# Four sums of weight blocks per seven-product pair: from VectorE subtractions to adding DMAs out of DRAM

## The chip, the core and the metric

The kernel runs on one core of one Trainium2 chip. The metric is the device time of one execution in microseconds (us). The engines named below are TensorE (PE; its weight loads PEld), VectorE (DVE), ScalarE (ACT), GpSimd (POOL) and SyncE (SP). SP only issues loads; POOL issues a few DMAs and does small masks. All arithmetic data is f32; matmul operands are f32 numbers that were rounded to the matmul's own format (`fp32r`).

## What is computed

A two-layer decoder trunk on 256 positions (two tiles of 128) with model width 2048. Layer 0 is a gMLP mixer, layer 1 a stick-breaking attention, each with a norm ahead, a residual add behind and a gate from the same input projection. Nearly all the work is in four products of the 256 x k activations with large weight matrices:

```python
proj = xn @ w_in                       # layer 0: 2048 -> 3*4096  (u | v | gate)
uv = jax.nn.gelu(proj[..., :2 * GMLP_WIDTH]); zg = proj[..., 2 * GMLP_WIDTH:]
...                                    # v: norm, causal mixing over positions
y = u * mixed * jax.nn.silu(zg)
h = h + y @ w_out                      # layer 0: 4096 -> 2048
proj = rms_norm(h) @ w_in              # layer 1: 2048 -> 4*2048  (q | k | v | gate)
...                                    # stick-breaking attention, 16 heads of 128
h = h + (o * jax.nn.silu(zg)) @ w_out  # layer 1: 2048 -> 2048
```

## The kernel before, in words

**Cutting.** Every weight tile comes from DRAM as f32 and is cut into two fp32r tiles: ACT copies it to `hi` (line 106), DVE subtracts `raw - hi` into `lo` (line 108). A product is then three matmuls, hi*hi, hi*lo and lo*hi (lines 112 to 114). There are five buffers of `hi` and five of `lo`, so the cutting can run at most five tiles ahead of PE.

**Pairs.** The two input projections run in pairs of column blocks of 512 (`Pair`). Of a pair's 16 k-tiles of 128 rows, 2*ks (ks is 4, in the gate/u stage 3) are taken by a Strassen-Winograd scheme: the 2x2 blocks left (2 row tiles by 2 k-groups) times right (2 k-groups by 2 column blocks) need seven block products, p1 to p7, in place of eight. The right-hand blocks b11, b12, b22, b21 are `ks` tiles of 128 x 512 each; they lie in SBUF in groups of two tiles (a group is 128 x 1024, with ks = 3 the second one is 128 x 512). The scheme needs four sums of right-hand blocks. `minus` (line 213) makes each on DVE, in place, one instruction a group. The left-hand sums s1 to s4 are made once a layer (`sums`). The other k-tiles of the pair are done plainly in `column(0)` and `column(1)`: one tile of 128 x 1024 is cut and used by twelve matmuls.

There are 19 pairs: v (3, layer 0, ks 4), gu (8, layer 0, ks 3), then in layer 1 qk (4), bv (2) and bg (2), with ks 4. The stages o (layer 0's output) and f (layer 1's) do plain products.

**Order.** `run` writes `head` (p1 and p5) in turn with the steps of the last pair's `column(1)`, then `body` (p6, p2, p7, p3, p4), then `column(0)`. A Tile scheduler with a timeline of its own sets the final order on each engine; each engine then takes its instructions strictly in that order. A load of a right-hand block into its buffer waits until the block's last reader in the pair before is done. The columns have three raw buffers (`wraw`). SP issues all these loads.

**Banks.** p1 goes to bank a, then b starts from a copy of a, p6 adds to b, c starts from a copy of b, and so on; an `es` tile on the side holds p5, which DVE adds to b and c (lines 243 and 250).

**Names in the rows.** `gu_b` is both a right-hand block (SBUF) and a bank (PSUM) of a gu pair; `gu_p_hi` and `gu_p_lo` are the cut of a block for one of the seven products; `gu_raw`, `gu_hi` and `gu_lo` belong to the columns; `vg` and `ws` are small tiles of layer 0's mixing, `gf` the last norm's gain. In the orders below the numbers stay on: `gu5_b00` is block b11 of pair gu5, `b01` is b12, `b11` is b22, `b10` is b21, and the last digit is the group.

Of the kernel before, what the change touches and what calls it, by code (L numbers as in the profile page):

```python
# [11 lines left out]
AF = mybir.ActivationFunctionType  # L12
ALU = mybir.AluOpType
# [11 lines left out]
def trunk_kernel(ctx: ExitStack, tc: tile.TileContext, x, xt, gcols, wst, a_w_in, a_v_norm_g,  # L25
# [11 lines left out]
    nc = tc.nc  # L37
# [45 lines left out]
    def f(ap):  # L83
        return ap.bitcast(F32)
# [31 lines left out]
    class Left:  # L116
# [10 lines left out]
        def sums(self, ks, out, name):  # L127

            full = []
            for i in range(2):  # L130
                sl = slice(i * ks, (i + 1) * ks)
                fl = sraw.tile([P, 4, S], F32, tag=f"b1{i + 1}_1", name=f"{name}_full{i}")
                nc.vector.tensor_add(fl[:, 0:ks], f(self.hi[:, sl, :]), f(self.lo[:, sl, :]))
                full.append(fl)
            a11, a12 = full[0][:, 0:ks, 0:P], full[1][:, 0:ks, 0:P]
            a21, a22 = full[0][:, 0:ks, P:S], full[1][:, 0:ks, P:S]
            sm = [sraw.tile([P, 2, 4, P], F32, tag=f"b2{i + 1}_1", name=f"{name}_sm{i}") for i in range(2)]
            s1, s2, s3, s4 = sm[0][:, 0, 0:ks], sm[0][:, 1, 0:ks], sm[1][:, 0, 0:ks], sm[1][:, 1, 0:ks]
            nc.vector.tensor_add(s1, a21, a22)
            nc.vector.tensor_sub(s3, a11, a21)  # L140
            nc.vector.tensor_sub(s2, s1, a11)
            nc.vector.tensor_sub(s4, a12, s2)
            for i, si in enumerate((s1, s2, s3, s4)):
                nc.scalar.copy(out[:, 0, i], si)
                nc.vector.tensor_sub(out[:, 1, i], si, f(out[:, 0, i]))
            self.s, self.ks = out, ks
# [32 lines left out]
    class Pair:  # L179
# [28 lines left out]
                tick(1)  # L208
                yield

        def minus(self, into, b0, b1):
            for g in range(len(self.groups)):
                nc.vector.tensor_sub(into[g], b0[g], b1[g])  # L213

        def head(self):
            left = self.left
            self.b11, self.b12 = self.load(0, 0), self.load(0, 1)
            self.a = self.bank("a")
            yield from self.block(self.b11, lambda k: left.part(k, 0), self.a, "p1", True)
            self.b22, self.b21 = self.load(1, 1), self.load(1, 0)  # L220
            self.minus(self.b11, self.b12, self.b11)
            self.e = self.bank("e")
            yield from self.block(self.b11, lambda k: left.sum_part(0, k), self.e, "p5", True)
            self.minus(self.b11, self.b22, self.b11)

        def body(self):
            left, off = self.left, self.left.ks
            b11, b12, b22, b21 = self.b11, self.b12, self.b22, self.b21
# [8 lines left out]
            nc.scalar.copy(es, e)  # L237
# [103 lines left out]
    left = Left(x_hi, x_lo)  # L341
# [87 lines left out]
    with ExitStack() as lg:  # L429
# [428 lines left out]
```

## Time and profile before

| | |
|---|---|
| median of 2 runs | 1185.88 us (1185.8 to 1185.95) |
| profiled execution | 1186.77 us, of which the profile's span is 1185.0 us |
| granted TensorE clock, mean | 0.995 |
| busy: PE, DVE, ACT, POOL | 1161.3, 945.3, 773.3, 40.6 us |
| DMA | 235.88 MB, mean 199 GB/s |
| subtractions of line 213 | 152 (v 24, gu 64, qk 32, bv 16, bg 16) |

The stages on the time axis: the first v products to about 60 us, the v pairs to about 160, gu pairs to about 510, stage o to about 720, the pairs of layer 1 to about 1080, stage f to the end. "DMA share" is the mean busy share of the core's 16 DMA engines. q1 is the queue that the loads go through, q0 the one of the DMAs that POOL issues.

### The profile page before, as it was taken

What the parts mean: (1) busy time and instruction counts of PE and PEld (TensorE: products, weight loads), DVE (VectorE), ACT (ScalarE), POOL (GpSimd) and SP (SyncE); (2) the same over time, 40 slices, a digit from 0 to 9 for tenths busy, and PEclk for the clock granted to TensorE, in tenths of its full rate; (3) what the DMA queues carried; (4) which work ended last, traced back from release to release, by engine and by line L of the source; (5) the groups of instructions that cost most, each with busy time, mean ns of one, the idle gap of its engine ahead of it and who ended that gap; (6) DMA issues with size and microseconds to landing.
All of it is one profiled execution on the core that took longest, in us unless ns stands there. A gap on an engine that the chain in (4) does not pass through costs nothing.

```text
span 1185.0 us, 14870 instructions
## 1 busy us (share of the span) xinstructions
PE 1161.3 (98%) x5393; PEld 961.3 (81%) x5393; DVE 945.3 (80%) x1050; ACT 773.3 (65%) x996; POOL 40.6 (3%) x55
## 2 busy tenths in 40 slices
PE   8799999999999999999999999999999999999997
PEld 6578888888888888888888887888888888878887
DVE  7599889989888887976556469899899989896564
ACT  6567668677676766766444456588679687885442
POOL 0200000110000000000000000001000000000000
PEclk9899999999999999999999999999999999999999
DMA  7975666675676566467555686475564564526662
GB/s 249 313 245 162 213 216 186 192 231 186 180 226 216 170 216 212 124 203 249 186 185 187 231 274 209 157 240 166 163 231 151 184 207 146 185 72 223 254 220 102
DMA packets 119609, 235.88 MB, mean 199 GB/s; under 512 B 7920, under 2 KB 12144, under 8 KB 119024
## 3 DMA queue, kind: packets, MB, share of 16 engines
q1 hardware_dynamic: 117648, 229.67, 59.5%
q0 software_dynamic: 1168, 4.20, 1.4%
q10 hardware_dynamic: 720, 1.07, 0.2%
q8 instruction: 42, 0.69, 0.2%
q14 instruction: 31, 0.25, 0.1%
HBM read 230.71 MB, written 4.19 MB: 198 GB/s over the span
## 4 chain that ended last, share of the span: by engine, by line
PE 78%; DVE 8%; ACT 6%; issue 4%; DMA 4%; SPq 0%; POOL 0%; POOLq 0%; DVEq 0%; ACTq 0%
PE o_acc L113 5%; PE o_acc L114 5%; PE o_acc L112 5%; PE gu_a L113 2%; PE gu_a L114 2%; PE gu_a L112 2%; DMA v_raw<-in_a_w_in 2%; PE gu_b L114 2%; PE gu_b L113 2%; PE gu_b L112 2%; PE f_acc L114 2%; PE f_acc L113 2%; PE f_acc L112 2%; PE gu_d L112 2%; PE gu_d L114 2%
## 5 line engine op out<-in xcount | busy, mean ns | idle before, releaser
L307 DVE TENSOR_TENSOR o_lo<-o_raw,o_hi 128x1024 fp32r<-128x1024 f32 x64 | 78.3, 1225 | 75.4 <-ACT o_hi L305 75.2
L106 ACT CAST gu_hi<-gu_raw 128x1024 fp32r<-128x1024 f32 x80 | 82.9, 1053 | 63.5 <-DMA gu_raw<-in_a_w_in 44.6
L305 ACT CAST o_hi<-o_raw 128x1024 fp32r<-128x1024 f32 x64 | 67.2, 1051 | 87.5 <-PE o_acc L114 65.0
L108 DVE TENSOR_TENSOR gu_lo<-gu_raw,gu_hi 128x1024 fp32r<-128x1024 f32 x80 | 96.7, 1223 | 30.0 <-ACT gu_hi L106 29.8
L106 ACT CAST gu_p_hi<-gu_b 128x1024 fp32r<-128x1024 f32 x112 | 91.5, 835 | 40.2 <-PE gu_c L114 22.6
L108 DVE TENSOR_TENSOR gu_p_lo<-gu_b,gu_p_hi 128x1024 fp32r<-128x1024 f32 x112 | 104.6, 957 | 4.9 <-ACT gu_p_hi L106 4.6
L112 PE MATMUL o_acc<-o_hi,yc 128*128 128x512 f32 x256 | 100.4, 392 | 0.0
L114 PE MATMUL o_acc<-o_hi,yc 128*128 128x512 f32 x256 | 99.8, 390 | 0.0
L113 PE MATMUL o_acc<-o_lo,yc 128*128 128x512 f32 x256 | 99.7, 389 | 0.0
L106 ACT CAST qk_p_hi<-qk_b 128x1024 fp32r<-128x1024 f32 x56 | 57.4, 1049 | 17.5 <-DVE qk_b L213 7.0
L108 DVE TENSOR_TENSOR qk_p_lo<-qk_b,qk_p_hi 128x1024 fp32r<-128x1024 f32 x56 | 67.2, 1223 | 1.0 <-ACT qk_p_hi L106 0.8
L108 DVE TENSOR_TENSOR v_lo<-v_raw,v_hi 128x1024 fp32r<-128x1024 f32 x40 | 48.5, 1227 | 24.2 <-ACT v_hi L106 24.1
L106 ACT CAST v_hi<-v_raw 128x1024 fp32r<-128x1024 f32 x40 | 41.4, 1048 | 35.1 <-DMA v_raw<-in_a_w_in 34.2
L213 DVE TENSOR_TENSOR gu_b<-gu_b,gu_b 128x1024 f32<-128x1024 f32 (+1 forms) x64 | 60.3, 955 | 0.4
L307 DVE TENSOR_TENSOR f_lo<-f_raw,f_hi 128x1024 fp32r<-128x1024 f32 x28 | 34.3, 1224 | 30.1 <-ACT f_hi L305 29.7
L114 PEld LDWEIGHTS o_acc<-o_hi,yc 128*128 128x128 f32 x256 | 48.1, 188 | 10.0
L112 PEld LDWEIGHTS o_acc<-o_hi,yc 128*128 128x128 f32 x256 | 48.1, 188 | 9.8
L113 PEld LDWEIGHTS o_acc<-o_lo,yc 128*128 128x128 f32 x256 | 48.1, 188 | 9.7
L112 PE MATMUL f_acc<-f_hi,y_hi 128*128 128x512 f32 (+1 forms) x160 | 55.6, 347 | 0.0
L114 PE MATMUL f_acc<-f_hi,y_lo 128*128 128x512 f32 (+1 forms) x160 | 55.6, 347 | 0.0
L113 PE MATMUL f_acc<-f_lo,y_hi 128*128 128x512 f32 (+1 forms) x160 | 55.5, 347 | 0.0
L106 ACT CAST v_p_hi<-v_b 128x1024 fp32r<-128x1024 f32 x42 | 42.9, 1049 | 14.4 <-DVE v_b L213 14.3
(491 smaller groups left out, 3372.1 us busy)
## 6 DMA issues: line engine op xcount, KB each, us to landing
gu_raw<-in_a_w_in SPq DMA_DIRECT2D x64, 512.0 KB, 4.4
o_raw<-in_a_w_out SPq DMA_DIRECT2D x64, 512.0 KB, 4.4
v_raw<-in_a_w_in SPq DMA_DIRECT2D x39, 512.0 KB, 5.2
gu_b<-in_a_w_in SPq DMA_DIRECT2D x32, 512.0 KB, 4.8
qk_b<-in_b_w_in SPq DMA_DIRECT2D x32, 512.0 KB, 5.2
qk_raw<-in_b_w_in SPq DMA_DIRECT2D x32, 512.0 KB, 3.9
f_raw<-in_b_w_out SPq DMA_DIRECT2D x32, 512.0 KB, 4.5
v_b<-in_a_w_in SPq DMA_DIRECT2D x24, 512.0 KB, 5.5
```

The costliest lines, as they stand in the source:

```text
L106: nc.scalar.copy(hi[:, 0:n], raw[:, 0:n])
L108: nc.vector.tensor_sub(lo[:, 0:n], raw[:, 0:n], f(hi[:, 0:n]))
L112: nc.tensor.matmul(acc, lh, hi, start=first, stop=False, skip_group_check=True)
L113: nc.tensor.matmul(acc, lh, lo, start=False, stop=False, skip_group_check=True)
L114: nc.tensor.matmul(acc, ll, hi, start=False, stop=last, skip_group_check=True)
L213: nc.vector.tensor_sub(into[g], b0[g], b1[g])
L305: nc.scalar.copy(hi, raw)
L307: nc.vector.tensor_sub(lo, raw, f(hi))
```

## The change

The four sums are no longer made on DVE. POOL issues a DMA with an adding operation: it reads a block of weights from DRAM a second time and adds it to the tile in SBUF. A DMA can add but not subtract, so the signs of some left-hand sums are turned, and two banks start from the negative of another bank (an ACT activation with scale -1 in place of a copy). Since a sum no longer needs the other blocks in SBUF, the body's products are in another order: p2, p6, p7, p3, p4.

```diff
-            nc.vector.tensor_add(s1, a21, a22)
-            nc.vector.tensor_sub(s3, a11, a21)
-            nc.vector.tensor_sub(s2, s1, a11)
+            nc.vector.tensor_sub(s1, a21, a22)
+            nc.vector.tensor_sub(s3, a21, a11)
+            nc.vector.tensor_sub(s2, a11, s1)
             nc.vector.tensor_sub(s4, a12, s2)
...
-        def minus(self, into, b0, b1):
-            for g in range(len(self.groups)):
-                nc.vector.tensor_sub(into[g], b0[g], b1[g])
+        def plus(self, into, i, j):
+
+            for g, (k, n) in enumerate(self.groups):
+                nc.gpsimd.dma_start(into[g], self.src(i * self.left.ks + k, n, j), accum_op=ALU.add)
 
         def head(self):
             left = self.left
-            self.b11, self.b12 = self.load(0, 0), self.load(0, 1)
+            self.x, self.y = self.load(0, 0), self.load(0, 1)
             self.a = self.bank("a")
-            yield from self.block(self.b11, lambda k: left.part(k, 0), self.a, "p1", True)
+            yield from self.block(self.x, lambda k: left.part(k, 0), self.a, "p1", True)
+            self.plus(self.x, 0, 1)
+            self.plus(self.y, 1, 1)
             self.b22, self.b21 = self.load(1, 1), self.load(1, 0)
-            self.minus(self.b11, self.b12, self.b11)
             self.e = self.bank("e")
-            yield from self.block(self.b11, lambda k: left.sum_part(0, k), self.e, "p5", True)
-            self.minus(self.b11, self.b22, self.b11)
+            yield from self.block(self.x, lambda k: left.sum_part(0, k), self.e, "p5", True)
+            self.plus(self.x, 1, 1)
 
         def body(self):
...
             b = self.bank("b")
-            nc.scalar.copy(b, a)
+            nc.scalar.activation(b, a, AF.Identity, scale=-1.0)
             es = jk.tile([P, CB], F32, tag="es", bufs=1, name=f"{self.name}_es")
             nc.scalar.copy(es, e)
-            block(b11, lambda k: left.sum_part(1, k), b, "p6")
+            block(self.b21, lambda k: left.part(off + k, 0), a, "p2")
+            block(self.x, lambda k: left.sum_part(1, k), b, "p6")
+            self.plus(self.x, 1, 0)
             c = self.bank("c")
             nc.scalar.copy(c, b)
-            self.minus(b12, b22, b12)
-            block(b21, lambda k: left.part(off + k, 0), a, "p2")
+            block(self.y, lambda k: left.sum_part(2, k), c, "p7")
             nc.vector.tensor_add(b, b, es)
-            block(b12, lambda k: left.sum_part(2, k), c, "p7")
+            block(self.b22, lambda k: left.sum_part(3, k), b, "p3")
             d = self.bank("d")
-            nc.scalar.copy(d, c)
-            self.minus(b11, b21, b11)
-            block(b22, lambda k: left.sum_part(3, k), b, "p3")
-            block(b11, lambda k: left.part(off + k, 1), d, "p4")
+            nc.scalar.activation(d, c, AF.Identity, scale=-1.0)
+            block(self.x, lambda k: left.part(off + k, 1), d, "p4")
```

So in the new kernel `x` (the buffer of b11) goes p1, add, p5, add, p6, add, p4; `y` (the buffer of b12) gets one add and is used by p7.

**POOL, in the middle of the gu stage.** Before, POOL has there only the loads of a small tile, one a pair; L94 belongs to the norm of layer 1:

```order
L441 DMA vg4_3216<-in_a_v_norm_g 128x512 [waits DMASW1_49,DVE_49]
L441 DMA vg5_3600<-in_a_v_norm_g 128x512 [waits DMASW4_49,DVE_49]
L441 DMA vg6_3984<-in_a_v_norm_g 128x512 [waits DMASW5_49,DVE_49]
L441 DMA vg7_4368<-in_a_v_norm_g 128x512 [waits DMASW6_49,DVE_49]
L94 TENSOR_TENSOR n1_r_6008<-n1_ms_6006,half_84 128x2 [waits DVE_49]
```

In the change it has, between two of these loads, the eight adds of pair gu5, the two of `y` first, then the three pairs on `x`:

```order
L441 DMA vg6_3984<-in_a_v_norm_g 128x512 [waits DMASW6_49,DVE_49]
L214 DMA gu5_b01_0_3354<-in_a_w_in 128x2x512 [waits DMAHW1_49,DMASW7_49,DVE_49]
L214 DMA gu5_b01_1_3356<-in_a_w_in 128x512 [waits DMAHW2_49,DVE_49]
L214 DMA gu5_b00_0_3350<-in_a_w_in 128x2x512 [waits DMAHW5_49,DMASW4_49,DVE_49]
L214 DMA gu5_b00_1_3352<-in_a_w_in 128x512 [waits DMAHW6_49,DMASW5_49,DVE_49]
L214 DMA gu5_b00_0_3350<-in_a_w_in 128x2x512 [waits DMASW1_49,DVE_49]
L214 DMA gu5_b00_1_3352<-in_a_w_in 128x512 [waits DMASW2_49,DVE_49]
L214 DMA gu5_b00_0_3350<-in_a_w_in 128x2x512 [waits DMASW3_49,DVE_49]
L214 DMA gu5_b00_1_3352<-in_a_w_in 128x512 [waits DMASW6_49,DMASW4_49,DVE_49]
L441 DMA vg7_4368<-in_a_v_norm_g 128x512 [waits DMASW7_49,DVE_49]
```

Each add on `x` waits for DVE's `lo` of the product that read the tile last; POOL goes from 60 instructions to 212.

**ACT, the same pair's body.** Before, p6 is cut ahead of p2, then p7, a copy between banks and p3 (L479 is the activation of the u block of the pair before):

```order
L106 CAST gu5_p60_hi_3505<-gu5_b00_0_3350 128x1024
L106 CAST gu5_p61_hi_3515<-gu5_b00_1_3352 128x512
L237 COPY gu5_es_3503<-gu5_e_3423 128x512
L106 CAST gu5_p20_hi_3526<-gu5_b10_0_3417 128x1024
L106 CAST gu5_p21_hi_3536<-gu5_b10_1_3419 128x512
L479 ACT_TABLE_LOAD
L479 ACTIVATE v_121<-gu4_b_3117,n0_r_340 128x512
L479 ACTIVATE v_121<-gu4_c_3138,n0_r_340 128x512
L106 CAST gu5_p70_hi_3544<-gu5_b01_0_3354 128x1024
L106 CAST gu5_p71_hi_3554<-gu5_b01_1_3356 128x512
L240 COPY gu5_c_3522<-gu5_b_3501 128x512
L106 CAST gu5_p30_hi_3565<-gu5_b11_0_3413 128x1024
```

In the change, with what each waits for (DMASW is a DMA that POOL issued):

```order
L106 CAST gu5_p20_hi_3507<-gu5_b10_0_3421 128x1024 [waits DVE_49,PE_49]
L106 CAST gu5_p21_hi_3517<-gu5_b10_1_3423 128x512 [waits DVE_49,PE_49]
L238 COPY gu5_es_3505<-gu5_e_3425 128x512 [waits PE_49]
L106 CAST gu5_p60_hi_3524<-gu5_b00_0_3350 128x1024 [waits DMASW3_49,DVE_49]
L106 CAST gu5_p61_hi_3534<-gu5_b00_1_3352 128x512 [waits DMASW4_49,DVE_49,PE_49]
L479 ACT_TABLE_LOAD
L479 ACTIVATE v_121<-gu4_b_3119,n0_r_340 128x512 [waits PE_49]
L479 ACTIVATE v_121<-gu4_c_3159,n0_r_340 128x512 [waits PE_49]
L106 CAST gu5_p70_hi_3545<-gu5_b01_0_3354 128x1024 [waits DMASW7_49,DVE_49]
L106 CAST gu5_p71_hi_3555<-gu5_b01_1_3356 128x512 [waits DMASW0_49,DVE_49,PE_49]
L106 CAST gu5_p30_hi_3563<-gu5_b11_0_3417 128x1024 [waits DVE_49,PE_49]
L106 CAST gu5_p31_hi_3573<-gu5_b11_1_3419 128x512 [waits DVE_49,PE_49]
```

p2 and p6 have changed places, and the cuts of p6 and p7 now wait for an adding DMA, as do those of p5, ahead of these rows, and of p4, behind them. All other cuts stand behind these in ACT's queue. DVE's instructions go from 1015 to 864, PE's from 5306 to 5304; ACT's and SP's counts stay.

More of the change, by code (lines that the diff above doesn't have):

```diff
@@ L209, in block @@
                 yield
-        def minus(self, into, b0, b1):
-            for g in range(len(self.groups)):
-                nc.vector.tensor_sub(into[g], b0[g], b1[g])
+        def plus(self, into, i, j):
+            for g, (k, n) in enumerate(self.groups):
+                nc.gpsimd.dma_start(into[g], self.src(i * self.left.ks + k, n, j), accum_op=ALU.add)
         def head(self):
             left = self.left
-            self.b11, self.b12 = self.load(0, 0), self.load(0, 1)
+            self.x, self.y = self.load(0, 0), self.load(0, 1)
             self.a = self.bank("a")
-            yield from self.block(self.b11, lambda k: left.part(k, 0), self.a, "p1", True)
+            yield from self.block(self.x, lambda k: left.part(k, 0), self.a, "p1", True)
+            self.plus(self.x, 0, 1)
+            self.plus(self.y, 1, 1)
             self.b22, self.b21 = self.load(1, 1), self.load(1, 0)
-            self.minus(self.b11, self.b12, self.b11)
             self.e = self.bank("e")
-            yield from self.block(self.b11, lambda k: left.sum_part(0, k), self.e, "p5", True)
-            self.minus(self.b11, self.b22, self.b11)
+            yield from self.block(self.x, lambda k: left.sum_part(0, k), self.e, "p5", True)
+            self.plus(self.x, 1, 1)
         def body(self):
             left, off = self.left, self.left.ks
-            b11, b12, b22, b21 = self.b11, self.b12, self.b22, self.b21
             def block(*args):
```

## The prediction

> **What bounds the kernel now.** I read the page's totals first, then the waits of PE, then stretches of a few stages.
>
> ```profile
> span 1185.0 us, 14870 instructions
> PE 1161.3 (98%) x5393; PEld 961.3 (81%) x5393; DVE 945.3 (80%) x1050; ACT 773.3 (65%) x996; POOL 40.6 (3%) x55
> q1 hardware_dynamic: 117648, 229.67, 59.5%
> q0 software_dynamic: 1168, 4.20, 1.4%
> ```
>
> PE is busy 98% of the span; but matmuls overlap, so I check it by its waits and its stretches.
>
> ```profile
> PE v_acc L112 <- ACT v_hi L106: 9.2, 4, 7.9
> PE v_acc L113 <- DVE v_lo L108: 1.5, 3, 0.7
> PE wps L74 <- DVE warm L71: 1.3, 1, 1.3
> PE O L695 <- ACT ah L688: 0.7, 1, 0.7
> ```
>
> These are PE's longest waits (us in total, times, longest). The first three belong to the opening of the kernel. The next view has, for a stretch, the length and the busy time of PE, PEld, DVE, ACT and POOL, then clock, DMA share and GB/s. The rows are the opening, the v pairs, the gu pairs, the pairs of layer 1, 40 us of stage o, and three short stretches.
>
> ```profile
> 0.00:20.00 20.00, 16.73 (x61) 10.42 (x62) 12.93 (x19) 11.01 (x17) 0.70 (x6) 1.00 0.72 237
> 20.00:40.00 20.00, 12.13 (x52) 9.47 (x50) 11.80 (x21) 14.84 (x32) 1.57 (x3) 0.91 0.78 264
> 40.00:60.00 20.00, 19.39 (x77) 15.00 (x77) 13.02 (x13) 11.01 (x17) 5.44 (x8) 0.92 1.00 346
> 70.10:152.20 82.10, 81.85 (x360) 67.23 (x359) 71.08 (x65) 56.45 (x77) 0.00 (x0) 1.00 0.64 205
> 190.80:491.90 301.10, 301.05 (x1376) 250.24 (x1375) 265.31 (x316) 207.71 (x263) 10.72 (x16) 1.00 0.65 202
> 724.90:1044.30 319.40, 317.21 (x1506) 263.38 (x1504) 292.39 (x318) 247.46 (x308) 19.33 (x18) 1.00 0.58 185
> 600.00:640.00 40.00, 40.00 (x181) 33.16 (x180) 20.68 (x19) 16.32 (x19) 0.00 (x0) 1.00 0.56 187
> 865.00:870.00 5.00, 5.00 (x25) 4.15 (x24) 5.00 (x8) 4.20 (x5) 0.00 (x0) 1.00 1.03 380
> 220.00:225.00 5.00, 5.00 (x24) 4.14 (x23) 5.00 (x9) 3.85 (x6) 0.00 (x0) 1.00 0.35 90
> 250.00:255.00 5.00, 5.00 (x27) 4.24 (x26) 4.62 (x6) 1.03 (x2) 1.04 (x2) 1.00 0.95 341
> ```
>
> In the pair stages DVE is busy 87% (71.08 of 82.10), 88% and 92%, nearly as much as PE, but PE's own gaps there are 0.25, 0.05 and 2.19 us. DVE is a near second and bounds nothing for long. PE loses 11.75 us in the first 60 us, to loads; the change doesn't touch those.
>
> **DVE's relief.** The subtractions that go:
>
> ```profile
> L213 DVE TENSOR_TENSOR gu_b<-gu_b,gu_b 128x1024 f32<-128x1024 f32 (+1 forms) x64 | 60.3, 955 | 0.4
> L213 DVE TENSOR_TENSOR qk_b<-qk_b,qk_b 128x1024 f32<-128x1024 f32 x32 | 38.6, 1221 | 0.1
> L213 DVE TENSOR_TENSOR v_b<-v_b,v_b 128x1024 f32<-128x1024 f32 x24 | 28.8, 1219 | 0.0
> L213 DVE TENSOR_TENSOR bg_b<-bg_b,bg_b 128x1024 f32<-128x1024 f32 x16 | 19.6, 1232 | 0.0
> L213 DVE TENSOR_TENSOR bv_b<-bv_b,bv_b 128x1024 f32<-128x1024 f32 x16 | 19.4, 1220 | 0.0
> ```
>
> That is 60.3 + 38.6 + 28.8 + 19.6 + 19.4 = 166.7 us of DVE, 152 instructions. All of it lies beside PE's work, so it is worth PE's gaps in the three stages at most: 0.25 + 0.05 + 2.19 = 2.5 us. I take all 2.5.
>
> **What the adds put on the DMA engines.** 152 adds. A pair with ks 4 adds four blocks of 4 x 128 x 512 x 4 bytes, 4.19 MB; a gu pair three quarters, 3.15 MB. That is 11 x 4.19 + 8 x 3.15 = 71.3 MB beside 235.88. The trace has no adding DMA. Its cheapest price is that of as many bytes loaded, its dearest that of two transfers of them, since the engine has to fetch the weights from DRAM and the tile from SBUF ahead of writing the sum. To see what this does, each stage's own traffic is needed. The starts of one ACT copy a pair give the periods:
>
> ```profile
> L237 ACT COPY gu_es<-gu_e x8: 579/580/588, 190.8 to 491.9; 128x512 f32<-128x512 f32 x8
> L237 ACT COPY qk_es<-qk_e x4: 569/575/589, 724.9 to 949.2; 128x512 f32<-128x512 f32 x4
> L237 ACT COPY v_es<-v_e x3: 574/577/578, 70.1 to 152.2; 128x512 f32<-128x512 f32 x3
> L237 ACT COPY bg_es<-bg_e x2: 576/583/590, 997.6 to 1044.3; 128x512 f32<-128x512 f32 x2
> ```
>
> v: 82.1 us for two pairs, 41.05 each, at 205 GB/s 8.42 MB. gu: 301.1 for seven, 43.0 each, at 202 GB/s 8.69 MB. Layer 1: 319.4 for seven, 45.6 each, at 185 GB/s 8.44 MB. What the engines can move: 380 GB/s over the best 5 us, 346 over 20 us with the share at 1.00, and by the mean packet of q1 229.67 MB in 59.5% of 1185 us, 326 GB/s.
>
> At one transfer a byte the pairs move 12.6, 11.8 and 12.6 MB: at 346 GB/s 36.4, 34.2 and 36.5 us, at 326 38.7, 36.3 and 38.8. All fit under 41.05, 43.0 and 45.6: nothing lost.
>
> At two transfers they move 16.8, 15.0 and 16.8 MB. At 380: 44.2, 39.4, 44.3 us, so 3.2 over in each of three v pairs and nothing elsewhere, 10 us in all. At 346: 48.6, 43.3, 48.6, so 3 x 7.5 + 8 x 0.3 + 8 x 3.0 = 49 us. At 326: 51.6, 46.0, 51.7, so 3 x 10.5 + 8 x 3.0 + 8 x 6.1 = 104 us.
>
> I take two transfers, because nothing in the operation spares the engine either fetch, and of the rates the middle between the best stretches, 10 and 49: 30 us. To this I add 1 us for each of the 8 gu pairs, which fit on average but not evenly: the queue's share is 0.35 in the stretch at 220 and 0.95 in that at 250, and an add that falls in the full part delays the column loads. Sum 38 us.
>
> The Trainium skill, in "Collectives: The Full Stack", section "The bandwidth ceiling: the fold count and why AG ≠ RS ≠ AR", says the same against this change: a DMA that adds reads two sources through one ring, and a reducing step measured 32.35 GB/s where a copying one measured 62.28, a ratio of 1.93. No run shown here has an adding DMA to compare with it.
>
> **What the adds put on the path of x.** `x` is now read, added to and read again three times a pair; before, DVE did this in 0.69 to 1.23 us a group. The tightest step is p6 to p4 in a gu pair. The view in order of time (start, length), for pair gu5:
>
> ```profile
> 403.92 1.05 ACT L106 CAST gu_p_hi<-gu_b 128x1024 fp32r<-128x1024 f32 x1 [0.80 <-PE gu_e L114]
> 405.01 1.23 DVE L108 TENSOR_TENSOR gu_p_lo<-gu_b,gu_p_hi 128x1024 fp32r<-128x1024 f32 x1 [0.23 <-ACT gu_p_hi L106]
> 412.07 0.39 PE L112 MATMUL gu_b<-gu_p_hi,xs 128*128 128x512 f32 x1
> 414.11 0.39 PE L112 MATMUL gu_a<-gu_p_hi,x_hi 128*128 128x512 f32 x1
> ```
>
> The first group of p6 is cut by 406.24 and PE begins it at 412.07, a lead of 5.8 us. Its nine matmuls take until 414.11, 0.227 us each. After the change p6, p7 and p3 lie between the cut of p6 and the use of p4: 27 matmuls, 6.1 us. So add, cut (1.05) and subtraction (1.23) have 6.1 + 5.8 = 11.9 us, the add itself 9.6; where ks is 4, 36 matmuls and 11.7. How long a DMA from POOL takes:
>
> ```profile
> gu_b<-in_a_w_in SPq DMA_DIRECT2D x32, 512.0 KB, 4.8
> vg<-in_a_v_norm_g POOLq DMA_DIRECT2D x8, 256.0 KB, 4.7
> gf<-in_final_g POOLq DMA_DIRECT2D x1, 1024.0 KB, 7.7
> L441 POOL DMA_DIRECT2D vg<-in_a_v_norm_g x8: 536/559/725, 39.1 to 415.2; - x8
> ```
>
> POOL's issue costs 0.56 us, 256 KB land in 4.7 and 1024 KB in 7.7 (4 us a MB of 1024 KB): 512 KB in 5.7, and with the second fetch of 512 KB 7.7, plus the issue 8.3. That fits into 9.6 with 1.3 us to spare, so this term is 0 in the sum. Its bounds: at 5.7 it is 0 too; at 12 us, with a full queue, 2.4 us in each gu pair and 0.3 in the others, 22 us. What hides it is the lead of the five buffers; where it is gone, ACT stands before the cut of p4, and behind it wait the column's cuts, the copies between banks and so PE. For p1 to p5 and p5 to p6 columns' steps of twelve matmuls (2.7 us) lie between, so these have more room.
>
> By the Trainium skill, "DMA: Bandwidth & Descriptors", section "Anatomy of one DMA — SWDGE (gpsimd) path", such a DMA takes about 2.0 us plus its bytes at 436 GB/s. By this 256 KB would land in 2.6 us; the row has 4.7, so the row decides.
>
> **The rest.** POOL: eight issues of 0.56 a pair, 4.5 us of 41; in the attention its masks stand among them, in the same order as ACT needs both, so 0. The two activations with scale -1 a pair lie on ACT, 65% busy; even at 1 us more each they would vanish there. The swap of p2 and p6 changes no matmul, and it gives the second add on `x` nine matmuls more of time. SP's loads are the same; b21 comes free earlier. Code on PE: two instructions fewer, 0.
>
> **Sum.** The profiled execution took 1186.8 us, 0.9 above the median of the runs. 1186.8 + 38 - 2.5 = 1222.3, on the scale of the median 1221 us, +3.0%.
>
> **Rivals.**
> - *Two transfers, as in the sum: 0.48.* Its own range goes from 1194 (10 us, less 2.5) to 1250 (49, with 8 of unevenness and some of the path's 22, less 2.5).
> - *The adds are hidden: 0.37.* The engine fetches both sources at once, an add costs a load, and the pairs stay at PE's pace. For it: the share of 0.58 to 0.65 leaves 35% and more. Against it: nothing shows such an overlap. Time 1185.9 - 2.5 = 1183, from 1178, if the opening gains too, to 1192. It holds up to the point where a pair's period is full: at 326 GB/s a v pair has room for 41.05 x 0.326 = 13.4 MB, less its own 8.42, which is 1.2 transfers of 4.19 MB; a pair of layer 1 for 14.9 less 8.44, 1.5 transfers.
> - *The engines work at the mean packet's rate, and the adds land late: 0.14.* 104 us of traffic plus 22 of the path, less 2.5: 1309 us. For it: the full stretch at 40 us, where the loads already make PE wait. Against it: 346 and 380 GB/s have been moved.
> - *PE gains more than its gaps: 0.01.* All its idle time of the opening and the stages is 11.75 + 2.5 = 14.3 us, 1.2%, so even then it is no gain over 2%.
>
> That the sums stay on DVE is excluded by the orders: the 152 adds stand on POOL.
>
> 2% (23.7 us, so 1162 to 1209.6) is about what a measurement of this kernel tells from no change. Faster by more: 0.01. Within: 0.37 of the second case and a quarter of the first, 0.11, in sum 0.48. Slower: 0.37 of the first and 0.14 of the third, 0.51. The range goes from 1178, the lowest of the hidden case, to 1290; above it lies a good half of the third case.
>
> **What would show it.** Right: DVE falls by some 165 us; q0 has about 75 MB, with a share of 30% or more (two transfers of 71.3 MB at 380 GB/s take 375 us, 32% of the span); the DMA share in the pairs is 0.9 and more; PE's gaps lie in the v pairs and layer 1 more than in gu; ACT's waits have DMAs on `v_b`, `qk_b`, `bv_b` and on the raw tiles. Wrong: q0's share near 20% with the pairs' periods unchanged (the adds were hidden), or gaps that are largest in the gu pairs, between p6 and p4, with a DMA share under 0.9 (then the path of `x` bounds, not the engines).

## The result, and the profile after

The changed kernel takes 1335.96 us (median of 2 runs, 1335.82 to 1336.11) against 1185.88: a ratio of 1.1261, 95% interval 1.1236 to 1.1287, so 150 us slower. The forecast was 1221 us with a range of 1178 to 1290: the direction of its likeliest case held, the size did not. The profile's totals after:

```profile
span 1334.4 us, 15107 instructions
PE 1214.1 (91%) x5393; PEld 979.9 (73%) x5393; DVE 797.7 (60%) x898; ACT 769.0 (58%) x995; POOL 200.7 (15%) x207
q1 hardware_dynamic: 117648, 229.67, 50.4%
q0 software_dynamic: 38416, 75.51, 32.4%
```

DVE is relieved of 147.6 us of busy time and 152 instructions, a little less than the 165 us foreseen. PE's idle time (span less busy) goes from 23.7 to 120.3 us, +96.6. But PE's busy time grows too, from 1161.3 to 1214.1, +52.8, with the same 5393 matmuls; 96.6 + 52.8 = 149.4 is the whole difference of the spans. q0 has the 71.3 MB more. In the chain of waits PE had 78% before and DMA 4%; now:

```profile
DMA 35%; PE 27%; issue 15%; ACT 11%; DVE 10%; POOL 1%; SPq 0%; ACTq 0%; POOLq 0%; DVEq 0%
```

The same stretches as before, v, gu and layer 1 (length, then busy PE, PEld, DVE, ACT, POOL, clock, DMA share, GB/s), and the starts of the copies that mark the pairs:

```profile
80.30:179.20 98.90, 87.31 (x363) 68.12 (x362) 53.17 (x48) 56.70 (x77) 18.98 (x16) 0.98 0.96 251
228.70:579.30 350.60, 320.79 (x1373) 255.67 (x1372) 219.44 (x261) 206.69 (x263) 68.94 (x72) 0.97 0.87 235
829.10:1189.20 360.10, 334.93 (x1502) 270.02 (x1503) 232.09 (x261) 244.06 (x306) 74.66 (x72) 0.96 0.94 243
...
L238 ACT COPY gu_es<-gu_e x8: 580/589/589, 228.7 to 579.3; 128x512 f32<-128x512 f32 x8
L238 ACT COPY qk_es<-qk_e x4: 579/584/593, 829.1 to 1086.0; 128x512 f32<-128x512 f32 x4
L238 ACT COPY v_es<-v_e x3: 576/580/589, 80.3 to 179.2; 128x512 f32<-128x512 f32 x3
L238 ACT COPY bg_es<-bg_e x2: 574/582/589, 1133.1 to 1189.2; 128x512 f32<-128x512 f32 x2
```

A v pair takes 98.9 / 2 = 49.4 us (before 41.05), a gu pair 350.6 / 7 = 50.1 (43.0), a pair of layer 1 360.1 / 7 = 51.4 (45.6). The first copy stands at 80.3 in place of 70.1, so the opening lost 10 us. Set one after the other, the marks give the 149.4 us: 10.2 up to the first copy, 27.7 in the v stage (80.3 to 228.7, before 70.1 to 190.8), 49.5 in gu, 16.8 from the last gu copy to the first qk copy, 40.7 in layer 1, 4.5 behind it. The DMA share in gu is 0.87, under the 0.9 that I had named as the mark of a bound by the engines.

PE's longest waits, then ACT's for the column loads of gu and for adding DMAs (us in total, times, longest):

```profile
PE v_acc L112 <- ACT v_hi L106: 21.4, 4, 11.8
PE gu_c L112 <- ACT gu_c L243: 9.9, 8, 3.8
PE v_c L112 <- ACT v_c L243: 9.7, 3, 3.9
PE gu_a L112 <- ACT gu_hi L106: 8.5, 6, 2.0
...
ACT gu_hi L106 <- DMA gu_raw<-in_a_w_in: 69.7, 21, 10.4
ACT gu_p_hi L106 <- DMA gu_b<-in_a_w_in: 64.4, 24, 5.9
ACT qk_p_hi L106 <- DMA qk_b<-in_b_w_in: 37.6, 10, 7.7
```

ACT, which takes its instructions in order, stands 64.4 us before cuts of gu blocks whose sum has not landed, 8 us a pair: 36.3 us before p5's first cut, 17.0 before p6's, 0.7 before p4's, and the rest before second groups. Behind such a cut stand the cuts of the columns and the copy of bank b to c (L243), and there PE waits. The column loads come late too: ACT's 69.7 us for them were 44.6 before, and they land in 8.2 us in place of 4.4. One gu pair shows where (start, length; first POOL's issues, then ACT's cuts, then DVE's subtraction):

```profile
413.41 1.18 POOL L214 DMA_DIRECT2D gu_b<-in_a_w_in  x1 [14.34 <-DVE gu_p_lo L108]
426.30 1.18 POOL L214 DMA_DIRECT2D gu_b<-in_a_w_in  x1 [10.27 <-DVE gu_p_lo L108]
...
423.70 1.05 ACT L106 CAST gu_p_hi<-gu_b 128x1024 fp32r<-128x1024 f32 x1 [5.27 <-DMA gu_b<-in_a_w_in]
433.68 1.05 ACT L106 CAST gu_p_hi<-gu_b 128x1024 fp32r<-128x1024 f32 x1 [2.15 <-DMA gu_b<-in_a_w_in]
...
411.90 1.22 DVE L108 TENSOR_TENSOR gu_p_lo<-gu_b,gu_p_hi 128x1024 fp32r<-128x1024 f32 x1
```

p1's first group is cut by 413.12. Its add goes out at 413.41, and p5's cut begins at 423.70, 10.6 us behind the end of p1's, after 5.27 us of standing. p6's cut (433.68) stands another 2.15 us for the second sum. For p4's cut, the third sum that I had called the tightest, ACT does not wait in this pair at all. The same place and pair in the trace of before, DVE's cut of p1, its subtraction and ACT's cut of p5:

```profile
346.49 1.22 DVE L108 TENSOR_TENSOR gu_p_lo<-gu_b,gu_p_hi 128x1024 fp32r<-128x1024 f32 x1
348.76 1.22 DVE L213 TENSOR_TENSOR gu_b<-gu_b,gu_b 128x1024 f32<-128x1024 f32 x1
...
352.41 1.05 ACT L106 CAST gu_p_hi<-gu_b 128x1024 fp32r<-128x1024 f32 x1
```

From the end of p1's cut (347.71) to p5's cut are 4.70 us; over the eight gu pairs it is 4.3 to 7.0, on average 5.4. The add that I had put at 8.3 us has to fit there.

### The profile page after: what moved, and what is told of

Read it like the earlier page. It is cut to its first block, busy times and chain, and to the rows that moved or that the text cites. A ratio compares the mean times of both kernels' runs of the same rounds, so it can differ in the third digit from the quotient of the medians.

```text
span 1334.4 us, 15107 instructions
## 1 busy us (share of the span) xinstructions
PE 1214.1 (91%) x5393; PEld 979.9 (73%) x5393; DVE 797.7 (60%) x898; ACT 769.0 (58%) x995; POOL 200.7 (15%) x207
## 3 DMA queue, kind: packets, MB, share of 16 engines
q1 hardware_dynamic: 117648, 229.67, 50.4%
q0 software_dynamic: 38416, 75.51, 32.4%
HBM read 302.01 MB, written 4.19 MB: 229 GB/s over the span
## 4 chain that ended last, share of the span: by engine, by line
DMA 35%; PE 27%; issue 15%; ACT 11%; DVE 10%; POOL 1%; SPq 0%; ACTq 0%; POOLq 0%; DVEq 0%
DMA gu_b<-in_a_w_in 12%; DMA v_raw<-in_a_w_in 5%; DMA qk_b<-in_b_w_in 4%; PE o_acc L113 4%; PE o_acc L114 4%; PE o_acc L112 4%; DMA bv_b<-in_b_w_in 3%; DMA v_b<-in_a_w_in 3%; DMA qk_raw<-in_b_w_in 3%; DMA bg_b<-in_b_w_in 2%; PE f_acc L114 2%; PE f_acc L113 2%; PE f_acc L112 2%; DVE gu_p_lo L108 2%; ACT gu_p_hi L106 1%
## 5 line engine op out<-in xcount | busy, mean ns | idle before, releaser
L106 ACT CAST gu_p_hi<-gu_b 128x1024 fp32r<-128x1024 f32 x112 | 90.9, 834 | 79.0 <-DMA gu_b<-in_a_w_in 64.4
L106 ACT CAST gu_hi<-gu_raw 128x1024 fp32r<-128x1024 f32 x80 | 82.7, 1047 | 79.2 <-DMA gu_raw<-in_a_w_in 69.7
L307 DVE TENSOR_TENSOR o_lo<-o_raw,o_hi 128x1024 fp32r<-128x1024 f32 x64 | 78.3, 1225 | 78.1 <-ACT o_hi L305 78.1
L214 POOL DMA_DIRECT2D gu_b<-in_a_w_in x64 | 66.7, 1106 | 275.2 <-DVE gu_p_lo L108 222.8
L214 POOL DMA_DIRECT2D qk_b<-in_b_w_in x32 | 39.1, 1222 | 351.1 <-DMA qk_b<-in_b_w_in 176.1
L106 ACT CAST qk_p_hi<-qk_b 128x1024 fp32r<-128x1024 f32 x56 | 57.1, 1050 | 42.8 <-DMA qk_b<-in_b_w_in 37.6
L108 DVE TENSOR_TENSOR v_lo<-v_raw,v_hi 128x1024 fp32r<-128x1024 f32 x40 | 48.4, 1222 | 48.8 <-ACT v_hi L106 48.6
L108 DVE TENSOR_TENSOR v_p_lo<-v_b,v_p_hi 128x1024 fp32r<-128x1024 f32 x42 | 50.5, 1222 | 40.6 <-ACT v_p_hi L106 40.5
L106 ACT CAST v_hi<-v_raw 128x1024 fp32r<-128x1024 f32 x40 | 41.5, 1047 | 51.9 <-DMA v_raw<-in_a_w_in 50.2
L114 PEld LDWEIGHTS o_acc<-o_hi,yc 128*128 128x128 f32 x256 | 48.1, 188 | 9.9
L112 PEld LDWEIGHTS o_acc<-o_hi,yc 128*128 128x128 f32 x256 | 48.1, 188 | 9.8
```

Source lines behind the costliest of these rows:

```text
L106: nc.scalar.copy(hi[:, 0:n], raw[:, 0:n])
L108: nc.vector.tensor_sub(lo[:, 0:n], raw[:, 0:n], f(hi[:, 0:n]))
L112: nc.tensor.matmul(acc, lh, hi, start=first, stop=False, skip_group_check=True)
L114: nc.tensor.matmul(acc, ll, hi, start=False, stop=last, skip_group_check=True)
L214: nc.gpsimd.dma_start(into[g], self.src(i * self.left.ks + k, n, j), accum_op=ALU.add)
L307: nc.vector.tensor_sub(lo, raw, f(hi))
```

## The experiments

Times are medians; where no interval stands, it is one run. "Period" is worked out as above, from the starts of the `es` copies; layer 1 is the mean over its seven distances.

| kernel | us | v | gu | layer 1 | first copy at |
|---|---|---|---|---|---|
| before | 1185.9 | 41.05 | 43.0 | 45.6 | 70.1 |
| changed | 1336.0 | 49.4 | 50.1 | 51.4 | 80.3 |
| e1 order, sums on DVE | 1195.7 | 41.8 | 43.2 | 46.4 | 68.1 |
| e2 bytes beside, v | 1222.7 | 49.1 | 43.3 | 46.5 | 70.7 |
| e3 the same, plain | 1200.0 | 43.5 | 43.3 | 46.5 | 66.8 |
| e4 plain in place of adds | 1219.9 | 43.0 | 43.4 | 47.0 | 78.3 |
| e5 narrow adds | 1214.2 | 42.1 | 43.2 | 46.6 | 73.5 |
| e6 narrow, twice | 1340.9 | 48.5 | 49.7 | 52.8 | 79.4 |
| e7 y's sum only | 1198.6 | 42.0 | 43.2 | 46.4 | 70.8 |
| e16 x's first sum only | 1240.2 | 43.6 | 44.6 | 49.1 | 76.0 |
| e17 x's third sum only | 1203.3 | 42.8 | 43.2 | 47.1 | 69.4 |
| e10 third on DVE | 1328.4 | 50.2 | 48.9 | 51.9 | 81.6 |
| e11 first on DVE | 1221.0 | 46.4 | 43.3 | 46.3 | 72.0 |
| e12 second on DVE | 1298.2 | 47.9 | 47.4 | 51.6 | 81.5 |

**The order alone (e1_order, e13_p2_back).** The sums come back to DVE, as additions; signs, activations and the new order stay.

```diff
-        def plus(self, into, i, j):
+        def plus(self, into, other):
-            for g, (k, n) in enumerate(self.groups):
-                nc.gpsimd.dma_start(into[g], self.src(i * self.left.ks + k, n, j), accum_op=ALU.add)
+            for g in range(len(self.groups)):
+                nc.vector.tensor_add(into[g], into[g], other[g])
```

> The changed kernel's product order (p2, p6, p7, p3, p4), signs and negative bank copies, but all four sums on DVE as tensor_add out of the blocks in SBUF; no adding DMA. If the adds' traffic or the wait for them is the cause, this is the kernel before within 5 us: 1181 to 1191 us, gu pairs 43 us apart. If the new order itself costs (the copy into bank c now stands behind the cuts of p3 on ACT), a good part of the 150 us is here: over 1200 us, with PE waiting for that copy.

1195.68 us, ratio 1.0084 [1.0068, 1.0101], between my two forecasts: the order costs 10 us without any adding DMA. PE's waits in e1:

```profile
PE v_c L112 <- ACT v_c L243: 2.7, 3, 1.1
PE gu_c L112 <- ACT gu_c L243: 2.0, 2, 1.3
PE qk_c L112 <- ACT qk_c L243: 1.8, 3, 0.7
PE bg_c L112 <- ACT bg_c L243: 1.4, 2, 0.9
```

All are for the copy of bank b to bank c. In the old order p2 stands between p6 and p7 and covers that copy; in the new one p7 follows p6 directly. e13 puts p2 back:

```diff
-            block(self.b21, lambda k: left.part(off + k, 0), a, "p2")
             block(self.x, lambda k: left.sum_part(1, k), b, "p6")
             ...
             nc.scalar.copy(c, b)
+            block(self.b21, lambda k: left.part(off + k, 0), a, "p2")
```

> The new signs and activations with all sums on VectorE, as in e1_order, but block p2 put back between p6 and p7. In the new order p7 follows right behind p6 and needs the copy of p6's bank, which ScalarE starts when p6 ends; in the old one p2 covered that copy. If this is where the order lost its 10 us, the time is back at 1184 to 1188 us and the waits of TensorE for the copy are gone; if the signs, the activations with -1 or the earlier p2 cost it, it stays at 1193 to 1197 us.

1186.79 us beside 1186.56, ratio 1.0001 [0.9991, 1.001]. The 10 us are the uncovered copy; signs and activations cost nothing.

**DVE's relief (e8_no_sums).** The kernel before without its sums, except in the qk pairs, and without anything in their place.

```diff
             for g in range(len(self.groups)):
-                nc.vector.tensor_sub(into[g], b0[g], b1[g])
+                if self.name[0:2] == "qk":
+                    nc.vector.tensor_sub(into[g], b0[g], b1[g])
```

> The kernel before with its sums of weight blocks left out (none made by any engine, except in the qk pairs): VectorE is relieved of about two thirds of the 167 us that the change takes from it, with no adding DMA and the old order. My forecast gave the relief 2.5 us in all: 1183 to 1186 us. If VectorE did hold the chain up: 1175 us or less.

1181.7 us, ratio 0.9964 [0.9953, 0.9976]: 4.4 us for 128.1 of the 166.7 us of subtractions, a little more than I had expected. So however the sums are made elsewhere, there is little more than these 4 us to gain.

**The price of the second fetch (e2_bytes_beside, e3_bytes_plain).** e1 with DMAs beside it in the v pairs, as many and as large as the sums, into six spare tiles that nobody reads: adding in e2, plain in e3 (without `accum_op`).

```diff
+                if spare and self.name[0] == "v":
+                    side = spare.pop(0)
+                    spare.append(side)
+                    nc.vector.tensor_copy(side[:, 0:n, 0:1], into[g][:, :, 0:1])
+                    nc.gpsimd.dma_start(side[:, 0:n], self.src(k, n, 0), accum_op=ALU.add)
```

> The order kernel (sums on DVE), and beside each sum of the three v pairs an adding DMA of the same size that POOL issues right behind the sum, into spare tiles that nothing reads. It loads the DMA engines as the change does, without anybody waiting for the adds; gu and layer 1 have none. If traffic is the cause: the v pairs go from 41.05 us to 46 or more (49.45 in the change) and the time to 1200 or more. If the wait for the sum is the cause: v pairs at 42 or less, time within 5 us of the order kernel.

> As the kernel with adds beside the v pairs, but the spare tiles are overwritten by plain DMAs of the same bytes, not added to. If an add costs two transfers a byte, this halves the extra traffic: q0's share halves, v pairs at 41 to 43 us by the traffic theory (12.6 MB a pair). If an add costs one transfer, v pairs are as with adds.

q0 in e1, then in e2, then in e3:

```profile
q0 software_dynamic: 1168, 4.20, 1.2%
```

```profile
q0 software_dynamic: 7696, 16.78, 6.9%
```

```profile
q0 software_dynamic: 4624, 16.78, 4.1%
```

The 12.58 MB more took 6.9% of 1220.7 less 1.2% of 1193.6 us, 69.9 us, as adds, and 34.8 us (4.1% of 1198.1, less the same) as plain copies: 5.55 and 2.77 us per MB, a ratio of 2.0. With nobody waiting for them the adds bring the v pairs to 49.1 us, nearly the change's 49.4; the plain ones to 43.5. So an adding DMA is two transfers, and in the v pairs this traffic alone is enough for what the change costs. It is not the only thing that is: two runs below have v pairs at 48.5 us with an eighth of the bytes (e6) and at 50.2 with three quarters of them (e10).

**Latency or bytes (e4_plain_in_path, e5_narrow_adds, e6_narrow_twice).** All three are the changed kernel with another transfer at line 214, in the same place and with the same waits. In e4 it is plain and overwrites the tile (the sums are left out):

```diff
-                nc.gpsimd.dma_start(into[g], self.src(i * self.left.ks + k, n, j), accum_op=ALU.add)
+                nc.gpsimd.dma_start(into[g], self.src(i * self.left.ks + k, n, j))
```

> The changed kernel with plain DMAs in place of the adding ones: x and y are overwritten and not added to, so the sums are left out; bytes from DRAM, POOL's issues, the waits and the order stay. If the second fetch is the cause: q0's share falls from 32 to 17% and the time to 1190 to 1215 us. If the path (issue, landing, the cut behind it) is: landings of 6 us and more stay and the time stays above 1260 us.

In e5 it adds 128 of 512 columns; in e6 two of 32 columns follow each other:

```diff
+                for _ in range(2):
+                    nc.gpsimd.dma_start(into[g][:, :, 0:32], self.src(i * self.left.ks + k, n, j)[:, :, 0:32],
+                                        accum_op=ALU.add)
```

> The changed kernel, each adding DMA brought to 128 of the 512 columns: the same 120-odd issues, waits and order, a quarter of the added bytes (17.8 MB in place of 71.3; three quarters of each sum are left out). If the traffic of two transfers a byte is what the change costs, nearly all of it goes: v pairs 42 to 43 us, gu pairs 43 to 44, layer-1 pairs 46 to 47, as with the plain DMAs (43.0, 43.4, 47.0), about 1200 to 1220 us in all. If the fixed part of an add's path (its issue of about 1.2 us on GpSimd and its landing) is what costs in the gu pairs, they stay at 47 us or more and the whole is over 1250. Matmul gaps gone, the granted clock should be back at 0.985 or more; if the clock fell for another reason than the gaps, it stays near 0.96.

> The changed kernel with two adding DMAs one behind the other, of 32 columns each, in place of each one of 512 (an eighth of the bytes, twice the issues, most of each sum left out): the path of each tile is two issues and two landings, some 9 to 12 us, with hardly any traffic. If latency in the chain add, cut, add is what costs in the gu pairs, they stand at 47 to 52 us and the whole at 1250 us or more, with adding DMAs ahead of the waiting cuts; if only the traffic costs, they stand at 43 to 44 us and the whole at 1200 to 1225 us.

e4 takes 1219.85 us and e5 1214.17, with landings of 4.7 to 6.6 and 4.2 to 5.9 us (landings count from the start of the issue): issues and waits stand where they do in the change, and the gu pairs lose nothing. e4 lies 5 us above what I had forecast for the second fetch as the cause. The 24 and 18 us that the two take more than e1 lie outside the gu pairs, 10 and 5 of them in the opening. e6 moves an eighth of the bytes, and takes 1340.9 us, 5 more than the change. Two adds in series, landing in 3.3 to 4.8 us each, do the same harm as one that lands in 7.6 to 9.0 in the change, though ACT stands longer before p6's first cuts (37 us in the gu pairs) than before p5's (26). In the same gu stretch of e6 the DMA share is low:

```profile
227.70:575.50 347.80, 320.08 (x1359) 258.93 (x1358) 220.27 (x261) 206.89 (x263) 125.49 (x127) 0.94 0.68 179
```

So the time between issue and landing can bring the whole loss with the engines at 0.68. That doesn't yet say that in the change it does.

**Bytes alone in the gu pairs (e9_gu_beside, e15_gu_beside_clean).** As e2, in the gu pairs, with two spare tiles.

```diff
+                if spare and self.name[0:2] == "gu":
+                    side, mark = spare[2 - n], spare[2].tile([P, 1], F32, tag="mark", name=f"{self.name}_mark")
+                    nc.vector.tensor_copy(mark, into[g][:, 0, 0:1])
+                    nc.gpsimd.tensor_copy(side[:, 0, 0:1], mark)
+                    nc.gpsimd.dma_start(side, self.src(k, n, 0), accum_op=ALU.add)
```

That is e15; in e9 DVE wrote to `side` itself, and so waited for the add before it, 46.9 us in all, which spoils e9 (1239.36 us, gu 48.7) as a test of bytes.

> The new order with all sums on VectorE, and beside it, in the gu pairs alone, adding DMAs of the same number and size as the changed kernel's (8 a pair, 3.1 MB) into two spare tiles that nobody reads. If the traffic of two transfers a byte is what costs the gu pairs 7 us each, they stand at 48 to 50 us here too, as the v pairs did in the same test; if it is the path of the adds (issue, landing, cut, one behind the other), they stay at 43.2 to 44 us, with their column loads landing in under 6 us.

> As e9_gu_beside, but VectorE no longer touches the spare tiles: it marks a small tile of its own, and GpSimd waits for the mark and for the spare tile to come free. Traffic in the gu pairs with nobody waiting for it. If the bytes alone cost the gu pairs their 7 us, they stand at 48 to 50 us; if the path of the sums does, at 43.2 to 44 us.

e15 takes 1244.54 us. Its first two gu pairs take 51.7 and 54.8 us; there PE waits 11.5 us for layer 0's mixing, whose small loads stand among the side adds on POOL. The last five, in one row:

```profile
299.90:540.30 240.40, 224.95 (x971) 179.47 (x969) 184.83 (x254) 144.47 (x179) 79.28 (x81) 0.98 0.91 242
```

240.4 / 5 = 48.1 us a pair, against 42.8 for the same five in e1. So the bytes alone cost 5.3 us a pair here, though nobody waits for them: in these five ACT waits 61.4 us for column loads (26.2 in e1). Whether all of it is the engines' doing is open: the adds also stand one behind the other on POOL, at other times than in the change.

**One sum at a time (e7_y_only, e16_first_only, e17_third_only; e10_third_on_dve, e11_first_on_dve, e12_second_on_dve).** The first three are e1 with one sum made by adds, 17.8 MB each; the others are the change with one of x's sums on DVE. As examples e16, from e1, and e11, from the change:

```diff
-            self.plus(self.x, self.y)
+            self.plus_dma(self.x, 0, 1)
```

```diff
-            self.plus(self.x, 0, 1)
+            self.plus_dve(self.x, self.y)
```

> The new order with one sum of the four (the one into y) made by adding DMAs, and the three into x on VectorE: 17.8 MB of adds, on the tile that has the longest time before it is read (two blocks lie between). Traffic: 17.8 MB at 5.5 us/MB is 98 us of DMA time beside the loads; per gu pair the sum of loads and adds is then under the pair's 43 us, so all is hidden: 1196 us, as with the new order alone, within 8 us. Path: nobody waits for y, the same 1196. [...]

> The new order with x's first sum alone (p1 to p5) made by adding DMAs, the other three on VectorE: a quarter of the added bytes, as in e7_y_only. Place: the trace of before has 4.2 us between the end of p1's first cut and p5's first cut, an add takes 1.2 us to issue and 5 to 7 to land, so ScalarE stands before p5's cut for 2 to 4 us in each pair, and the gu pairs go from 43.2 to 45 to 47 us, the layer-1 pairs up as well: 1212 to 1245 us. Bytes: as e7_y_only, 1196 to 1201 us, gu pairs 43.2.

> The new order with x's third sum alone (p6 to p4) made by adding DMAs, the other three on VectorE, the same bytes again. My forecast gave it 9.6 us and called it the tightest; in e11 its adds landed just ahead of p4's cut. Place: it fits, 1196 to 1202 us, gu pairs 43.2 to 43.6. If it is as tight as the first sum, over 1210 us.

> The changed kernel with x's third sum (block p6 to block p4, the only one I gave a price in the forecast) on VectorE and the other three by adding DMAs. Traffic: a quarter of the added bytes goes, so the v pairs fall from 49.4 to about 43 to 45 us, in this and in the next two kernels alike, and the gu pairs by some 1.8 us. Path: if this sum is the tight one, the gu pairs come back to 43 to 45 us; if not, they stay over 47 us.

> The changed kernel with x's first sum (block p1 to block p5) on VectorE and the other three by adding DMAs. Between the two blocks there lies only the previous pair's last column. Traffic: as with the third sum. Path: gu pairs over 47 us if the third sum is the tight one, 43 to 45 us if it is this one.

> The changed kernel with x's second sum (block p5 to block p6, with block p2 between) on VectorE and the other three by adding DMAs. Traffic: as with the third sum. Path: gu pairs over 47 us if another sum is the tight one; 43 to 45 us if it is this one. If each of the three kernels gives back two to three us a gu pair, no one sum is the cause, but the chain of all three.

With equal bytes the sum into y gives 1198.55 us (ratio 1.0104 [1.0088, 1.012]), x's third 1203.28 (1.0139 [1.012, 1.0157]) and x's first 1240.22 (1.045 [1.0432, 1.0467]). Against e1's 1195.7 the first costs 44.5 us, y's 3 and the third 8; e17 is 1 us above its forecast, e16's gu pairs 0.4 below. In e16 ACT waits for the first sum once in each gu pair:

```profile
ACT gu_p_hi L106 <- DMA gu_b<-in_a_w_in: 32.5, 8, 5.1
```

That is 4.1 us a time, of 9.0 from the end of p1's cut to p5's cut; 1.4 us a pair of it reaches PE, the rest is taken up by the lead of the cuts. (The 4.2 us in the forecast of e16 are from p5 to p6 in the old order; I had taken that place for p1 to p5.) The place also sets how long an add takes. Landings in e16, then in e17 (KB each, median us):

```profile
gu_b<-in_a_w_in POOLq DMA_DIRECT2D x8, 512.0 KB, 8.1
gu_b<-in_a_w_in POOLq DMA_DIRECT2D x8, 256.0 KB, 9.1
```

```profile
gu_b<-in_a_w_in POOLq DMA_DIRECT2D x8, 512.0 KB, 5.8
gu_b<-in_a_w_in POOLq DMA_DIRECT2D x8, 256.0 KB, 5.9
```

The same sizes take 2 to 3 us longer between p1 and p5. While e16's adds are under way, other DMAs take 0.42 of the engines on average, in e17 0.10. In the program the loads of b22 and b21 stand at the first place; that these are the ones that delay the adds is argued, not shown.

From the other side, DVE taking back the third sum gives back 7.5 us, the second 37.8, the first 115.0, all with the same quarter of the bytes gone. The v pairs did not fall to 43 to 45 us in any of the three, as I had expected from the traffic: they stand at 50.2 (third), 47.9 (second) and 46.4 (first). In e11's gu stretch PE loses 1.5 us of 302.8, at a DMA share above the change's 0.87:

```profile
209.00:511.80 302.80, 301.31 (x1376) 250.43 (x1375) 232.89 (x275) 207.81 (x263) 55.78 (x58) 1.00 0.91 253
```

At equal bytes the gu pairs take 43.3 us in e11, 48.9 in e10 and 47.4 in e12. So with three sums made by adds the place decides, not the mean load of the engines, and the first sum's place is the dear one. For all four sums this isn't shown: the change moves a third more adds than e11, and in e15 as many bytes as the change's cost 5.3 us a pair by themselves.

**The clock (e14_filled_gaps).** A good part of PE's extra busy time in the change is time at half clock: the clock record has 103.3 us at 0.5 in 18 stretches (before 14.2 in 2), and PE is busy in 70.6 us of them (before 3.9). One of them, by three stretches of 3.4 us:

```profile
318.30:321.70 3.40, 1.52 (x6) 0.70 (x4) 1.16 (x2) 2.08 (x3) 0.00 (x0) 1.00 0.65 202
321.70:325.10 3.40, 3.28 (x8) 2.61 (x9) 3.40 (x5) 3.40 (x5) 2.94 (x3) 0.50 0.34 90
325.10:328.50 3.40, 3.40 (x17) 2.80 (x16) 2.32 (x3) 1.38 (x3) 0.14 (x1) 1.00 1.00 180
```

In the first PE is busy for less than half; in the second it runs 8 matmuls at clock 0.5; in the third 17 at full clock. e14 is the change with eight matmuls of zero weights ahead of each gu pair's first column:

```diff
+                if spare and self.name[0:2] == "gu" and j == 0 and i == 0:
+                    for _ in range(8):
+                        nc.tensor.matmul(banks[0], spare[0], self.hi[:, 0, :], start=False, stop=False,
+                                         skip_group_check=True)
```

> The changed kernel with 8 matmuls with zero weights ahead of the first column of each gu pair (they add zero to a bank, 8 x 0.227 = 1.8 us of work for each pair, 14.5 us in all). In the change four of the eight gu pairs had a gap of 2 to 3 us at this place, and each time a stretch of 3.4 us at half clock behind it. If the half clock comes from TensorE being idle for 2.0 us or more of a stretch of 3.41 us, those four stretches are gone, which saves 1.7 us each, and where the added work lies in gaps it costs nothing: 1322 to 1340 us. If the half clock has another cause, the stretches stay, and the time is 1336 to 1350 us.

1333.21 us (1329.7 to 1334.8). Between the first and the last gu copy the change has five stretches at half clock that begin behind the first pair (321.7, 359.3, 410.5, 461.7 and 560.6 us); e14 has none there. Its stretch from the first to the last gu copy:

```profile
229.60:572.40 342.80, 323.49 (x1430) 261.02 (x1429) 219.47 (x261) 206.69 (x264) 69.52 (x72) 0.99 0.90 240
```

It is 7.8 us shorter than the change's 350.6 with 56 matmuls more in it (8 in each of 7 pairs; the clock 0.99 in place of 0.97). This execution is the fastest of the four; the medians of the whole kernels differ by 2.8 us. Added work made the stage faster, so the half clock follows from the gaps. In all PE is busy 67 us more at half clock than before; by halving, that is an estimated 33 us of the change's 150.

## Why the prediction was wrong

**What bounds the kernel, DVE's relief: right.** PE bound it, and the relief was worth little: 4.4 us where I took 2.5. That the change does not touch the opening was wrong: the opening lost 10.2 us.

**Two transfers a byte: right.** The ratio is 2.0 (e2 and e3). In the change the adds took 32.4% of 1334.4 less 1.4% of 1185 us for 71.3 MB, 5.83 us per MB, the loads 50.4% of 1334.4 us for 229.67 MB, 2.93. The 1.93 that the Trainium skill states in "Collectives: The Full Stack", section "The bandwidth ceiling: the fold count and why AG ≠ RS ≠ AR", was measured on collectives; the 2.0 here, on DMAs from DRAM into SBUF, agrees with it. The rival that the adds are hidden is out.

**The rate: mis-sized.** I took the middle between 380 and 346 GB/s. By the prices just given a v pair needs 8.42 x 2.93 + 4.19 x 5.83 = 49.1 us of the engines, and takes 49.4; a layer-1 pair needs 49.2, a gu pair 25.5 + 18.4 = 43.8. So the end at 346 (48.6, 43.3, 48.6) was the right one, and a little cheap. The sum over the pairs by these prices is 3 x 8.0 + 8 x 0.8 + 8 x 3.6 = 59 us, where I put 30. And a gu pair that needs 43.8 of 43.2 us doesn't cost 0.8 or my 1 us, but 5.3 where the bytes were tried alone (e15): the engines reached a share of 0.91 there, not 1. For a v pair the agreement of 49.1 with 49.4 is in part luck, since e10 needs 43.0 by the same prices and takes 50.2.

**The path of x: the step that failed.** I priced p6 to p4 at 0 and let p1 to p5 go with the words that column steps lie between, "so these have more room". They had less: in the gu pairs of the trace of before ACT comes to p5's cut 4.3 to 7.0 us behind the end of p1's, and in e1, which has the new order, 5.7 us on average against 7.1 from p6 to p4. I had also counted the room up to PE's use of the block. Counted so, p1 to p5 had 8.5 to 11.3 us in the trace of before, and the add would have seemed to fit; but ACT stands from the moment it comes to the cut, and all cuts behind it come late. My estimate of an add, 8.3 us, was about right for this place: 8.1 in e16 for two tiles, the issue included, which I had added once too often. Put into the right gap (8.3 less 5.4) it would have shown ACT standing some 3 us in each gu pair; e16 measured 4.1. At p6 to p4 the price of 0 held in the gu pairs: they stand at 43.2 us in e17, as in e1. In e16 the first sum alone costs 44.5 us over e1: by the table about 7.9 in the opening, 3 x 1.8 in v, 8 x 1.4 in gu and 8 x 2.7 in layer 1.

**How they go together.** The first sum alone costs 44.5 us over e1, the other three together 25.3 (e11), all four 140.3. So 70 us belong to the meeting of both: more bytes, later landings, a longer stand before p5 and p6, gaps, half clock. A division of the gu pairs' 7 us into bytes and path can't be given, since each alone loses some (5.3 in e15, 1.4 in e16). For layer 1 the bytes alone were not tried.

**The order: missed.** "The swap of p2 and p6 changes no matmul" is so, but p2 was the cover of a copy. It cost 10 us where I had 0.

**POOL's issues: mis-sized.** I had 0.56 us from the plain loads of `vg`. The adding ones, shortest, median, longest:

```profile
L214 POOL DMA_DIRECT2D gu_b<-in_a_w_in x64: 874/1181/1392, 196.3 to 586.4; - x64
L214 POOL DMA_DIRECT2D qk_b<-in_b_w_in x32: 1185/1204/1713, 748.3 to 1089.1; - x32
```

It is twice that for two tiles. The landings above contain it.

**The rivals.** The third, engines at the mean rate and adds landing late, gave 1309 us and was the nearest. Its 22 us for the path were too low, and for the wrong place; whether its 104 us for the bytes were too high isn't shown, since bytes alone cost 27 us over e1 in the v pairs (e2) and 5.3 us in each of five gu pairs (e15), and layer 1 was not tried. That the largest loss would be in the gu pairs with a share under 0.9 was named as the mark of the path: gu lost most (49.5 us) at 0.87, though a v pair lost more (8.4) than a gu pair (7.1). The place between p6 and p4 was the wrong one.

## What to carry to other kernels

Where an operation gets slower, list all the places it stands in, with the time from the end of its input to the start of its user, and compare the longest duration with the shortest of these, not with the one that looks tight in the order. Where the user's engine takes its work in order, count up to the moment it comes to the user, not to the one when the last consumer needs the result. An adding DMA costs the engines two transfers and its user a landing; put it only where a whole block of work lies between, as y's sum did (3 us for 17.8 MB). When a block of matmuls moves, ask which copies it was covering.

## What the runs showed of the hardware

**The granted clock goes by fixed stretches.** All stretches at half clock begin on a grid of 3.413 us that runs on through the whole execution. I counted PE's idle time in each such stretch of all nineteen runs (6869 stretches; gaps between starts of matmuls, less 0.227 us): each of the 225 with more than 2.1 us of idle time was followed by a stretch at half clock, and of the 6618 with less than 1.98 all but nine were followed by full clock. It may be the sum of several gaps: in the stretch from 318.30 above PE idles 2.3 us in two gaps, the longer of 1.4. Half clock makes a matmul of 512 columns start every 0.427 us in place of 0.227. So idle time of 2.1 us costs up to 1.7 us more, if it falls into one stretch. The Trainium skill, "TensorE: Matmul & The Clock Gate", Part 1, states the free-running window of 3413 ns, and the trace agrees. Its rule in the section "HAM oscillation — how this bites in real kernels", that no gap may be longer than about 3.4 us, differs from the count here, where 2.1 us within one window were enough; the measurement decides.

**The issue of an adding DMA** takes POOL 1.2 us for two tiles of 128 rows and 0.88 for one, against 0.72 and 0.55 for the plain ones in their place in e4.
